# A mixture of 32 experts: the experts ordered on chip by their tokens, the 20 lightest four at a time in 32-slot column tiles

## The chip, the core and the metric

The kernel runs on one core of a Trainium2 chip. The core has a tensor engine (PE, with weight loads shown apart as PEld), a vector engine (DVE), a scalar engine (ACT), GpSimd (POOL), and SyncE (SP), which here issues the transfers; 16 DMA engines ("the rings") carry them. The metric is the device time of one execution in microseconds (us). A lower one is better.

## What the reference computes

Two transformer layers with attention mixers, feed-forward layers and norms over 256 tokens of 1024 features, in fp32, and at the end of the second layer a mixture of 32 experts (4 groups of 8). Each token takes the best group and in it the best two experts. All of the change lies in this mixture (shortened here):

```
pg_top, g_idx = lax.top_k(softmax(t @ w_rg + b_rg), 1)          # the group
le_sel = le[group g_idx of t @ w_re + b_re]
pe_top, e_idx = lax.top_k(softmax(le_sel), TOP_K)               # TOP_K = 2 of its 8 experts
pe_top = pe_top / jnp.sum(pe_top, axis=-1, keepdims=True)
flat_idx = g_idx * EXPERTS_PER_GROUP + e_idx
cw = jnp.sum(one_hot(flat_idx, 32) * (pg_top * pe_top)[..., None], axis=1)
for e in range(N_EXPERTS):
    he = jax.nn.silu(t @ w1e[e]) * (t @ w3e[e])                 # 1024 -> 256
    out = out + cw[:, e:e + 1] * (he @ w2e[e])                  # 256 -> 1024
```

So 512 pairs of token and expert are computed. The number of tokens of an expert follows from the inputs: with these, the heaviest have 34 and 33 tokens; of experts 6 to 31 the seventh heaviest has 21.

## The kernel before

The instructions are written in Python with a tile scheduler that orders each engine's instructions; pools of buffers with a tag ("ps", "we", ...) decide when a buffer can be reused. The mixture stage is `moe` with `moe_round`. It starts at about 1361 us of the span.

*Routing.* `moe` computes the router's choice on DVE, the number of tokens ahead of each token at its expert (a product with a triangle of ones into `pk`; its columns 64 to 95 are the tokens of each expert), the rank `rk` (token by expert: the slot of the token there, or a number far off) and the weights `cw`. If an expert has over 64 tokens, `n_more` further rounds follow; here there are none.

*Slots.* Each expert has CAP = 64 slots. `one_hot` makes for four experts the 0/1 matrix of tokens against 4 x 64 slots. `gather(qd)` multiplies the tokens (in a high and a low part, `hhi` and `hlo`) with it: `gT`, the tokens of four experts feature-major, in banks of the tag p0, read back by ACT and DVE.

*Passes.* There are N = 16 passes of two experts. `up(n)` multiplies the gathered tokens with w1 and w3: for each expert the 64 columns of `gT` are the stationary operand and go to 64 of PE's 128 columns, so that two experts stand beside one another and fill a bank (`ph`, tag p1) of 128 slots by 512. Behind it ACT and DVE form silu times the other half. `mid(n)` transposes the result and the slots' matrix; `down(n)` multiplies with w2, also two experts beside one another, into two banks; `scatter(n)` adds the slots' rows back to their tokens in four banks that stay for the whole stage. The order is written out by hand:

```
gather(0)
up(0)
for n in range(N):
    if n + 1 < N:
        up(n + 1)
    if n % 2 == 0 and n + 2 < N:
        gather(n // 2 + 1)
    mid(n)
    if n:
        scatter(n - 1)
    down(n)
```

*Weights.* An expert has 3 MB: two halves of w1|w3 together (`w13[e, 0]`, `w13[e, 1]`) and `w2e[e]`. Each MB is one transfer into a tile `we`, issued on SP. `expert_load(i)` gives the i-th MB in order of use, to a ring of 18 tiles from five pools; the first 18 are issued before the stage, the rest each when the tile's former contents (18 loads ago) have been used. All addresses are constants. The last two w2 come in four halves.

Of the kernel before, what the change touches and what calls it, by code (L numbers as in the profile page):

```python
# [33 lines left out]
KD = 8  # L34
# [5 lines left out]
CAP = 64  # L40
# [124 lines left out]
def interleave(gens, width, other=iter(()), every=1):  # L165
    """emit the steps of some units of work in turn, `width` units at a time, and every so often one of `other`"""
    gens, live, n = list(gens), [], 0
    while gens or live:
        while gens and len(live) < width:
            live.append(gens.pop(0))  # L170
        for g in list(live):
            if next(g, live) is live:
                live.remove(g)
            n += 1
            if n % every == 0:
                next(other, None)
    for _ in other:
        pass


class Net:
# [124 lines left out]
    def rope_steps(self, pool):  # L306
        """the rotary tables, as steps"""
# [41 lines left out]
    def split_w(self, src, n, cut=D, lo=None):  # L349
        """weights as hi and lo parts; returns col -> (hi, lo) accessor for column ranges within a half"""  # L350
# [31 lines left out]
    def split_a(self, src, pool=None, tag=None):  # L382
        """hi and lo parts of a [P, S] activation"""
# [37 lines left out]
    def prep(self, k, g):  # L421
        """operands of the next projection from the k-th chunk of x; the norm's factor comes later"""
# [20 lines left out]
    def bcast(self, cols, tag="p3"):  # L443
        """[P tokens, 2] factors -> [P, 2 * P tokens] on every partition (PSUM)"""
# [5 lines left out]
    def bcast_heads(self, out, cols):  # L450
        """[P tokens, (2, 2)] factors of two heads -> [(2 heads, 64), 2 * P tokens]"""
# [17 lines left out]
    def ffn(self, name, layer, post, side):  # L469
        """side(pool): steps of other work to lay between the chunks"""  # L470
# [56 lines left out]
    def feat(self, src, pairs, sink, count, tags=("p3",), lo=None):  # L527
        """feature-major projections, 128 columns at a time"""
# [10 lines left out]
    def gelu(self, out, h, k=1.0):  # L539
        """from x / 2: x * (1 + tanh(sqrt(2 / pi) * (x + 0.044715 * x**3))) / 2"""  # L540
# [29 lines left out]
    def rope_apply(self, raw, outs, key="h", swap=ROPE_SWAP):  # L570
        """outs: (tile slice, first partition, partitions)"""
# [52 lines left out]
    def out_proj(self, src, ys, post, order=tuple(range(KD))):  # L624
        """output projection: columns 0-511 accumulate as the chunks of ys come, in the given order"""
# [18 lines left out]
    def even_early(self):  # L644
        """what the even mixer needs that depends on weights and shapes only"""
# [212 lines left out]
    def odd_early(self):  # L858
        """the odd mixer's keys, with zeros for the other heads' features"""
# [127 lines left out]
    def ada_round(self, r, pool):  # L987
        """2048 of the modulation's columns, from c alone, as steps"""
# [27 lines left out]
    def prep_final1(self, k):  # L1016
        """sums of squares for the two norms that follow the last feed-forward of block 1"""
# [5 lines left out]
    def block2_early(self):  # L1023
        """operands of the third block that depend on weights alone, as steps"""
# [73 lines left out]
    def block2(self, post):  # L1098
        nc, A = self.nc, self.A
        rest = self.block2_in()  # L1100
        with self.tc.tile_pool(name="b2", bufs=1, reuse_waits="tile") as bp:
# [11 lines left out]
            def second(yl):  # L1113
                """the products with p_b, times their gates"""
# [155 lines left out]
    def lru_decay(self):  # L1270
        """4 * softplus(-lam) and its negative"""
# [61 lines left out]
    def rwkv_in(self, c, rkv, w2a, tw, half, hold):  # L1333
        """decays, keys and their products for two heads"""
# [92 lines left out]
    def pair_room(self, c, j):  # L1427
        """room for a unit in the weights' rings, which two units share"""
# [148 lines left out]
    def moe_pre(self):  # L1577
        """what the router needs besides x"""
# [11 lines left out]
        nc.sync.dma_start(self.lc, bass.AP(tensor=A["b_r"].tensor, offset=A["b_r"].offset, ap=[[0, P], [1, 36]]))  # L1590
        p = self.bank("p2")
# [4 lines left out]
    def post2(self, d, p, u):  # L1596
        """the mixers' part of x; router sums and token-major copies, without the norm's factor"""
# [21 lines left out]
    def keep_warm(self, n):  # L1619
        """products that nothing reads, so that the tensor engine's clock stays up while it waits"""  # L1620
# [4 lines left out]
    def moe(self, final):  # L1625
# [9 lines left out]
        with self.tc.tile_pool(name="moe", bufs=1, reuse_waits="tile") as mp:  # L1635
# [34 lines left out]
            def first_max(a, mx, shape):  # L1670
                """one-hot of the first of the largest entries"""
# [35 lines left out]
            self.rk = t(2, 32, keep=True)  # L1707
# [13 lines left out]
            self.tt(f2(self.rk), pk[:, 0:64], big, OP.add)  # L1721
# [23 lines left out]
            self.cw = t(2, 32, keep=True)  # L1745
# [7 lines left out]
            for i in range(3):  # L1753
                self.ts(th[:, i:i + 1], cm, CAP * (i + 1) + 0.5, op0=OP.is_gt)
# [5 lines left out]
            self.moe_round()  # L1760
            final()
            n_more = nc.values_load(nxi[0:1, 0:1], min_val=0, max_val=3)
            with self.tc.For_i(0, n_more, 1):
                rf = self.rk[:, :, :].rearrange("p j e -> p (j e)")
                self.ts(rf, rf, -float(CAP), op0=OP.add)
# [3 lines left out]

    def expert_open(self):  # L1770
        self.pre = self.es.enter_context(self.tc.tile_pool(name="pre", bufs=1, side="right", reuse_waits="tile"))
        self.rings, self.loads, self.ahead = [], 0, []
# [7 lines left out]
    def expert_ahead(self, n=99):  # L1780
        """start the loads of up to n more MB"""
        for _ in range(min(n, len(self.rings) - self.loads)):
            self.ahead.append(self.expert_load(self.loads))

    def expert_load(self, i):
        """the i-th MB of the experts' weights, in order of use: two experts' w1|w3 halves each time, and the w2 of the two before"""
        i %= 3 * NEXP
        if i < 4 or i >= 3 * NEXP - 2:
            n, i = (0, i) if i < 4 else (NEXP // 2 - 1, i - 3 * NEXP + 6)
        else:  # L1790
            n, i = (i - 4) // 6, (i - 4) % 6
            if i < 4:
                n += 1
# [325 lines left out]
```

## Time and profile before

| what | us |
|---|---|
| median of three timed runs | 1645.82 (1641.7 to 1648.69) |
| span of the profiled execution | 1641.5 |
| mixture stage, in the span | 1361 to 1641.5 |
| of it the 16 passes | 1376 to 1620 |

The profile is of one execution, and the page gives its span; its own device time lies around the span by some tenths of a us at most, as the fastest timed run of 1641.7 beside it shows. A row of the timeline has start, duration, engine, line of the kernel, operation, output and inputs by the program's names, and partitions x elements; "x16" are records that stand together, and in brackets is the idle time ahead and what ended it. fp32 products leave two records each. "SPq" is SP's queue of issues. The granted clock is a share of PE's full speed (2.4 GHz; 0.5 is 1.2).

### The profile page before, as it was taken

The page shows a single profiled execution, that of the slowest core. Times are in us where ns is not written, and L with a number is a line of the kernel's source. Part 1 is how long each engine was busy: PE and PEld are TensorE (multiplying, and loading weights), DVE is VectorE, ACT ScalarE, POOL GpSimd, SP SyncE. Part 2 cuts the span into 40 slices and gives each one's busy share as a digit, 9 for nine tenths or more (in the row PEclk, how much of TensorE's full clock was granted, in tenths as well). Part 3 has the DMA queues.
Part 4 walks back from the last instruction along what each step waited for, and adds up shares of the span by engine and source line. Part 5 has one row for each costly group of instructions (what it writes and reads, how often), then busy time and mean ns, then how long its engine had stood idle before and what let it go on. Part 6 is the DMA issues. An engine that isn't in the chain of part 4 may idle for free.

```text
span 1641.5 us, 29942 instructions
## 1 busy us (share of the span) xinstructions
PE 1580.0 (96%) x12048; PEld 1389.5 (85%) x12048; DVE 1069.2 (65%) x1964; ACT 709.7 (43%) x1263; POOL 321.0 (20%) x340
## 2 busy tenths in 40 slices
PE   8999998999999999999999999998999989999996
PEld 8999996789999999999879999997888886445443
DVE  6787776777876578757987777657875474323223
ACT  5544444545444444444554446544474332112112
POOL 4121222122221112112122221243231130000000
PEclk9999999999999999999999999999999999999998
DMA  8675554136765567555334775453431297999950
GB/s 300 246 276 197 202 195 156 52 129 212 276 217 174 187 234 275 207 172 185 116 107 163 271 269 180 142 203 105 156 116 53 81 377 291 405 422 420 387 205 28
DMA packets 61041, 344.33 MB, mean 210 GB/s; under 512 B 10976, under 2 KB 15200, under 8 KB 26848
## 3 DMA queue, kind: packets, MB, share of 16 engines
q1 hardware_dynamic: 58080, 340.65, 56.7%
q8 instruction: 96, 1.57, 0.4%
q0 software_dynamic: 640, 1.57, 0.4%
q10 hardware_dynamic: 2176, 0.13, 0.1%
q14 instruction: 49, 0.40, 0.1%
HBM read 339.05 MB, written 2.36 MB: 208 GB/s over the span
## 4 chain that ended last, share of the span: by engine, by line
PE 69%; issue 18%; DVE 8%; POOL 2%; ACT 2%; DMA 1%; SPq 0%; ACTq 0%; DVEq 0%; POOLq 0%
PE ps L232 68%; DVE l L238 2%; PE ps L235 1%; ACT h L257 1%; POOL rte L238 1%; DVE xl L247 0%; DVE t L238 0%; DVE xh L242 0%; POOL t L238 0%; DMA s<-in_ev_win 0%; DVE t L247 0%; POOL sq L238 0%; POOL kne L238 0%; DVE x L238 0%; DMA x<-in_xT 0%
## 5 line engine op out<-in xcount | busy, mean ns | idle before, releaser
L232 PE MATMUL ps<-xh,h 128*128 128x256 f32 x1992 | 568.3, 285 | 12.0 <-ACT h L257 5.9
L232 PE MATMUL ps<-xl,h 128*128 128x256 f32 x1992 | 567.2, 285 | 0.3
L232 PE MATMUL ps<-xh,l 128*128 128x256 f32 x1992 | 567.2, 285 | 0.2 <-DVE l L238 0.2
L257 ACT ACTIVATE h<-s 128x1024 fp32r<-128x1024 f32 (+4 forms) x419 | 401.4, 960 | 367.5 <-PE ps L232 289.1
L238 DVE TENSOR_TENSOR l<-s,h 128x1024 fp32r<-128x1024 f32 (+4 forms) x416 | 465.6, 1127 | 136.7 <-ACT h L257 135.2
L232 PEld LDWEIGHTS ps<-xh,h 128*128 128x128 f32 x1992 | 377.6, 190 | 17.0 <-ACT h L257 6.2
L232 PEld LDWEIGHTS ps<-xh,l 128*128 128x128 f32 x1992 | 378.6, 190 | 6.0 <-DVE l L238 1.9
L232 PEld LDWEIGHTS ps<-xl,h 128*128 128x128 f32 x1992 | 378.5, 190 | 1.7 <-DVE xl L247 1.1
L232 PE MATMUL ps<-ah,h 128*128 128x256 f32 x704 | 201.5, 286 | 0.0
L232 PE MATMUL ps<-ah,l 128*128 128x256 f32 x704 | 199.3, 283 | 0.1
L232 PE MATMUL ps<-al,h 128*128 128x256 f32 x704 | 199.1, 283 | 0.0
L238 POOL TENSOR_TENSOR t<-t,t 128x256 f32<-128x256 f32 x93 | 119.4, 1284 | 400.3 <-DVE t L238 340.8
L232 PEld LDWEIGHTS ps<-ah,l 128*128 128x128 f32 x704 | 134.9, 192 | 0.4 <-DVE l L238 0.3
L232 PEld LDWEIGHTS ps<-al,h 128*128 128x128 f32 x704 | 135.0, 192 | 0.0
L232 PEld LDWEIGHTS ps<-ah,h 128*128 128x128 f32 x704 | 134.9, 192 | 0.0
L232 PE MATMUL ps<-we,gT 128*64 128x512 f32 x512 | 122.9, 595 | 0.0
L238 DVE TENSOR_TENSOR t<-ps,rb 128x256 f32<-128x256 f32 x196 | 81.9, 420 | 33.2 <-PE ps L232 25.1
L232 PEld LDWEIGHTS ps<-we,gT 128*64 128x64 f32 x512 | 37.7, 137 | 71.3 <-issue 69.3
L257 ACT ACTIVATE ah<-t 128x256 fp32r<-128x256 f32 x88 | 36.7, 417 | 114.4 <-POOL t L238 114.4
L238 DVE TENSOR_TENSOR al<-t,ah 128x256 fp32r<-128x256 f32 x88 | 37.9, 431 | 61.8 <-ACT ah L257 61.8
L247 DVE SCALAR_TENSOR_TENSOR ada<-s,ca,ada 128x1024 f32<-128x1024 f32 x56 | 71.5, 1277 | 0.0
L238 POOL TENSOR_TENSOR sa<-sa,sq 128x256 f32<-128x256 f32 x34 | 41.8, 1230 | 149.9 <-ACT sq L257 149.4
(462 smaller groups left out, 2207.6 us busy)
## 6 DMA issues: line engine op xcount, KB each, us to landing
s<-in_ffn_gu SPq DMA_DIRECT2D x87, 1024.0 KB
we<-in_w SPq DMA_DIRECT2D x64, 1024.0 KB
s<-in_ffn_dn SPq DMA_DIRECT2D x64, 704.0 KB
we<-in_w2e SPq DMA_DIRECT2D x30, 1024.0 KB
s<-in_w_ada SPq DMA_DIRECT2D x24, 1024.0 KB
s<-in_w_in SPq DMA_DIRECT2D x18, 1024.0 KB
s<-in_w_ada_f SPq DMA_DIRECT2D x8, 1024.0 KB
s<-in_ev_win SPq DMA_DIRECT2D x7, 1024.0 KB
```

Source lines behind the costliest of these rows:

```text
L232: self.nc.tensor.matmul(out, lhsT, rhs, start=start, stop=stop, skip_group_check=True)
L235: self.nc.tensor.transpose(out, in_, ident)
L238: return (eng or self.nc.vector).tensor_tensor(out, a, b, op=op)
L247: self.nc.vector.scalar_tensor_tensor(out, a, s, b, op0=op0, op1=op1)
L257: self.nc.scalar.activation(out, a, f, **kw)
```

## The change

The 16 passes become 11: six of two experts with 64 slots for the positions 0 to 11, and five of four experts with 32 slots for 12 to 31. A position is not an expert's number any more: positions 0 to 5 are experts 0 to 5 (NFIX = 6), and behind them stand the others by their tokens, the heaviest first. `expert_order` computes this on DVE: a key of tokens x 32 less the number, for each expert how many keys are larger (its position), the one-hot `eq` of it, `ex` with the expert's number in it, and the permutation `perm`. `turn` then has two PE operations, which give each position's expert number (`idx`, copied as int32) and the transposed `rc` (ranks and weights); `place` multiplies with `perm`, for ranks and weights by position, `rcP`. From position 6 on, a weight load takes its address from a register: `value_load` reads `idx` into a register of SP (52 times, once for w13 and once for w2 of each position). A new `expert_list` gives the order of loads. `n_more` also counts if the seventh heaviest of experts 6 to 31 has over 32 tokens. Three small DVE operations in `moe_pre` prepare constants; docstrings are taken out. The sizes of the ring, the bytes and everything ahead of the stage stay. The core of the diff:

```diff
+NFIX, NWIDE = 6, 12
+PASSES = [(p, 2, 64) for p in range(0, NWIDE, 2)] + [(p, 4, 32) for p in range(NWIDE, NEXP, 4)]
...
-            self.rk = t(2, 32, keep=True)
+            self.rc = T("rc", (P, 4, 32))
+            self.rk, self.cw = self.rc[:, 0:2], self.rc[:, 2:4]
...
+            order = self.expert_order(T, pk[:, 64:96])
+            tn = t(3)
+            for i in range(3):
+                self.ts(tn[:, i:i + 1], self.top8[:, NWIDE - NFIX:NWIDE - NFIX + 1], 1024 * (i + 1) + 0.5, op0=OP.is_gt)
+            self.tt(th, th, tn, OP.max)
...
+    def expert_order(self, T, cnt):
...
+        self.stt(key, cnt, 32.0, iota, op0=OP.mult, op1=OP.subtract)
+        nc.vector.max(self.top8, key[:, NFIX:])
+        self.ts(key[:, 0:NFIX], iota[:, 0:NFIX], -1.0, 1.0e6, op0=OP.mult, op1=OP.add)
+        w = self.tmp("t2")
+        wq = w[:, 0:P].rearrange("p (q e) -> p q e", e=32)
+        self.tt(wq, idv, q4(key), OP.mult)
+        nc.vector.tensor_reduce(kp, w[:, 0:P], axis=AX.X, op=OP.add)
+        self.ts(gt, key, kp, op0=OP.is_gt)
+        nc.vector.tensor_reduce(pos, gt, axis=AX.X, op=OP.add)
+        self.ts(eq, iota, pos, op0=OP.is_equal)
+        self.ts(ex, eq, self.ei, op0=OP.mult)
+        perm = w[:, P:2 * P]
+        self.tt(perm.rearrange("p (q e) -> p q e", e=32), q4(eq), self.e4.unsqueeze(2).to_broadcast([P, 4, 32]), OP.mult)
+        def turn():
+            self.po = self.bank("p1")
+            self.mm(self.po[:, 0:32], self.ones[0:32, :], ex[0:32, :])
+            self.tr(self.po[:, P:2 * P], self.rc.rearrange("p a e -> p (a e)"), self.ident)
+            nc.vector.tensor_copy(self.idx, self.po[:, 0:32])
+            nc.vector.tensor_copy(rcT, self.po[:, P:2 * P])
+
+        def place():
+            self.mm(self.po[:, 2 * P:3 * P], rcT, perm)
+            nc.vector.tensor_copy(self.rcP.rearrange("p a e -> p (a e)"), self.po[:, 2 * P:3 * P])
...
+    def expert_list(self):
+
+        up = [[(0, p + i, h) for h in range(2) for i in range(n)] for p, n, _ in PASSES]
+        dn = [[(1, p + i, 0) for i in range(n)] for p, n, _ in PASSES]
+        return up[0] + up[1] + dn[0] + up[2] + dn[1] + dn[2] + up[3] + sum((u + d for u, d in zip(up[4:], dn[3:])), []) + dn[-1]
...
+        if p < NFIX:
+            src = self.A["w2e"][p] if kind else self.A["w13"][p, h]
+        else:
+            if (p, kind) not in self.where:
+                self.where[p, kind] = self.nc.sync.value_load(self.idx[0:1, p:p + 1], min_val=0, max_val=NEXP - 1)
+            e = bass.ds(self.where[p, kind], 1)
+            src = self.A["w2e"][e].squeeze(0) if kind else self.A["w13"][e, h].squeeze(0)
+        if kind and p >= PASSES[-1][0]:
+            self.late.append((t, src))
+            if len(self.late) == PASSES[-1][1]:
+                for c in range(2):
+                    for o, a in self.late:
+                        self.nc.sync.dma_start(o[:, c * D:(c + 1) * D], a[:, c * D:(c + 1) * D])
...
-            for k in range(KD):
-                for ee in range(2):
-                    c = (2 * (n % 2) + ee) * 64
-                    self.mm(ph[ee * 64:ee * 64 + 64, :], gT[k][:, c:c + 64],
-                            w[2 * ee + k // 4][:, (k % 4) * 512:(k % 4 + 1) * 512], k == 0, k == KD - 1)
+            for h in range(2):
+                w = self.expert_get(*[(0, p + i, h) for i in range(m)])
+                for k in range(4):
+                    for i in range(m):
+                        c = n % 2 * P + i * cap
+                        self.mm(ph[i * cap:(i + 1) * cap, :], gT[4 * h + k][:, c:c + cap], w[i][:, k * 512:(k + 1) * 512], h == 0 and k == 0, h == 1 and k == 3)
...
-                    for ee in range(2):
-                        self.mm(py[ee * 64:ee * 64 + 64, :], heT[:, f * P + ee * 64:f * P + ee * 64 + 64],
-                                w[ee][:, nn * D + f * 512:nn * D + (f + 1) * 512], f == 0, f == 1)
+                    for i in range(m):
+                        self.mm(py[i * cap:(i + 1) * cap, :], heT[:, f * P + i * cap:f * P + (i + 1) * cap],
+                                w[i][:, nn * D + f * 512:nn * D + (f + 1) * 512], f == 0, f == 1)
...
-        N = NEXP // 2
+        N = len(PASSES)
         gather(0)
+        turn()
         up(0)
+        place()
```

The order of instructions on PE at the start of the stage, before: gather(0)'s products (stationary `oh`) with the first products of up(0) (stationary `gT`, moving `we`) between them.

```order
L232 MATMUL ps_16976<-oh_3166_16910,hlo_16902 128x256
L232 MATMUL ps_16998<-we_16260,gT_16946 64x512
L232 MATMUL ps_16998<-we_15207,gT_16947 64x512
L232 MATMUL ps_16998<-we_16260,gT_16947 64x512
L232 MATMUL ps_16998<-we_15207,gT_16948 64x512
L232 MATMUL ps_16987<-oh_3165_16909,hhi_16899 128x256
L232 MATMUL ps_16987<-oh_3165_16909,hlo_16901 128x256
```

The same place of the change: the end of gather(0), the two operations of `turn` (`moe_ex`, `moe_rc`), and then up(0) from its first product.

```order
L233 MATMUL ps_17011<-oh_3167_16916,hlo_16908 128x256
L233 LDWEIGHTS ones
L233 MATMUL ps_17022<-moe_ex,ones 128x32
L236 MATMUL ps_17022<-con,moe_rc 128x128
L233 MATMUL ps_17027<-we_15207,gT_16970 64x512
L233 MATMUL ps_17027<-we_15209,gT_16970 64x512
L233 MATMUL ps_17027<-we_15207,gT_16971 64x512
```

All of gather(0) now stands ahead of up(0), with the products of `turn` between the two.

A down on PE before, in the middle of the stage: two banks (17519 and 17526) one after the other, two experts (`we`) in turn.

```order
L232 MATMUL ps_17519<-we_17515,t_3293_17493 64x512
L232 MATMUL ps_17519<-we_17517,t_3293_17493 64x512
L232 MATMUL ps_17519<-we_17515,t_3293_17493 64x512
L232 MATMUL ps_17519<-we_17517,t_3293_17493 64x512
L232 MATMUL ps_17526<-we_17515,t_3293_17493 64x512
```

A down of a narrow pass of the change: two banks (18030, 18041) and four experts (`we_17986`, `_17997`, `_18008`, `_18019`).

```order
L233 MATMUL ps_18030<-we_17986,t_3353_17964 32x512
L233 MATMUL ps_18041<-we_17986,t_3353_17964 32x512
L233 MATMUL ps_18030<-we_17997,t_3353_17964 32x512
L233 MATMUL ps_18041<-we_17997,t_3353_17964 32x512
L233 MATMUL ps_18030<-we_18008,t_3353_17964 32x512
L233 MATMUL ps_18041<-we_18008,t_3353_17964 32x512
L233 MATMUL ps_18030<-we_18019,t_3353_17964 32x512
L233 MATMUL ps_18030<-we_17986,t_3353_17964 32x512
L233 MATMUL ps_18030<-we_17997,t_3353_17964 32x512
```

The two banks alternate for the first three experts, so that neighbouring products there have the same expert and the same columns of PE.

SP's order in the change, where the loads by register begin (`ISA` are register operations); before, this is a row of DMA issues with nothing between.

```order
L1864 DMA we_16812<-in_w2e 128x2048
L1854 TENSOR_LOAD moe_idx
L1854 ISA x2
L1864 ISA
L1864 DMA we_17223<-in_w 128x2048
L1854 TENSOR_LOAD moe_idx
L1854 ISA x2
L1864 ISA
L1864 DMA we_17234<-in_w 128x2048
```

Ahead of each load of a new expert stand a TENSOR_LOAD and three register operations on SP.

## Rows read from the trace of the kernel before

**Rows 1.** The page: span, and busy time of each engine (share of the span, instructions).

```profile
span 1641.5 us, 29942 instructions
PE 1580.0 (96%) x12048; PEld 1389.5 (85%) x12048; DVE 1069.2 (65%) x1964; ACT 709.7 (43%) x1263; POOL 321.0 (20%) x340
```

**Rows 2.** Windows: length, PE, PEld, DVE, ACT, POOL busy, clock, DMA share, GB/s.

```profile
1370.00:1380.00 10.00, 10.00 (x55) 5.07 (x55) 5.31 (x29) 4.66 (x8) 0.00 (x0) 1.00 0.19 64
...
1405.00:1435.00 30.00, 30.00 (x169) 15.35 (x169) 9.25 (x22) 5.44 (x11) 0.00 (x0) 1.00 1.01 423
1435.00:1465.00 30.00, 30.00 (x170) 15.33 (x170) 9.25 (x22) 5.42 (x11) 0.00 (x0) 1.00 1.01 421
...
1376.00:1622.00 246.00, 243.55 (x1301) 119.77 (x1299) 71.24 (x168) 43.99 (x81) 0.23 (x1) 1.00 0.82 333
...
1582.00:1584.00 2.00, 1.92 (x10) 0.91 (x12) 0.84 (x3) 0.00 (x0) 0.00 (x0) 1.00 0.21 86
```

**Rows 3.** Timeline of PE and its weight loads, 1450 to 1475 us (start, duration).

```profile
1454.38 3.65 PE L232 MATMUL ps<-we,t 128*64 128x512 f32 x16
...
1454.86 0.14 PEld L232 LDWEIGHTS ps<-we,t 128*64 128x64 f32 x2 [0.29 <-issue]
...
1457.86 7.04 PE L232 MATMUL ps<-we,gT 128*64 128x512 f32 x32
...
1465.56 0.28 PE L232 MATMUL ps<-t,yh 128*128 128x256 f32 x1
1465.68 0.28 PE L232 MATMUL ps<-t,yl 128*128 128x256 f32 x1
```

**Rows 4.** Timeline of SP: issues of weight loads in the mixture stage.

```profile
1377.45 3.79 SPq L1805 DMA_DIRECT2D we<-in_w  x2
...
1428.06 0.80 SPq L1805 DMA_DIRECT2D we<-in_w2e  x2
...
1458.06 1.58 SPq L1805 DMA_DIRECT2D we<-in_w2e  x2
...
1574.15 2.92 SPq L1803 DMA_DIRECT2D we<-in_w2e  x4
```

**Rows 5.** Waits of SP, 1325 to 1641 us: total, times, longest.

```profile
SPq L1805 <- PE ps L232: 168.8, 44, 14.6
```

**Rows 6.** Timeline of DVE around the first gather.

```profile
1370.95 0.48 DVE L242 TENSOR_SCALAR gT<-ps,mod 128x256 f32<-128x256 f32 x1
...
1371.60 0.41 DVE L238 TENSOR_TENSOR oh<-con,moe_r 128x256 fp32r<-128x256 f32 x1
...
1372.52 0.15 DVE L1757 CAST moe_nxi<-t 128x1 int32<-128x1 f32 x1
...
1372.92 0.47 DVE L242 TENSOR_SCALAR gT<-ps,mod 128x256 f32<-128x256 f32 x1
```

**Rows 7.** Timeline of PE around the first gather.

```profile
1375.17 0.39 PE L232 MATMUL ps<-oh,hhi 128*128 128x256 f32 x1
...
1376.33 12.23 PE L232 MATMUL ps<-we,gT 128*64 128x512 f32 x54
```

**Rows 8.** Timeline of all engines at the end.

```profile
1616.34 3.65 PE L232 MATMUL ps<-we,t 128*64 128x512 f32 x16
...
1629.84 3.12 SPq L1938 DMA_DIRECT2D out<-o  x5
```

**Rows 9.** Instructions of line 1762, and of tile we: ns min/median/max, first and last start.

```profile
L1762 SPq TENSOR_LOAD <-moe_nxi x1: 468/468/468, 1577.1 to 1577.1; - x1
L1762 SPq FUSED_REGOPS  x1: 186/186/186, 1577.7 to 1577.7; - x1
...
L1805 SPq DMA_DIRECT2D we<-in_w x64: 327/328/1755, 1197.8 to 1563.2; - x64
```

**Rows 10.** A window of an earlier stage, and PE's timeline in it.

```profile
1200.00:1210.00 10.00, 7.75 (x29) 4.55 (x28) 9.06 (x22) 9.44 (x18) 2.62 (x4) 0.83 0.51 205
...
1206.27 1.96 PE L232 MATMUL ps<-t,rgw 128*128 128x256 f32 x4 [1.00 <-DVE t L247]
```

More of the change, by code (lines that the diff above doesn't have):

```diff
@@ L1744, in moe @@
             self.tt(w2, w1, e2, OP.mult)
-            self.cw = t(2, 32, keep=True)
             for j in range(2):
@@ L1758, in moe @@
             es.close()
-            self.moe_round()
+            self.moe_round(*order)
             final()
@@ L1763, in moe @@
             with self.tc.For_i(0, n_more, 1):
-                rf = self.rk[:, :, :].rearrange("p j e -> p (j e)")
-                self.ts(rf, rf, -float(CAP), op0=OP.add)
+                self.ts(self.rk, self.rk, -64.0, op0=OP.add)
+                for c, cap in ((slice(0, NWIDE), 64.0), (slice(NWIDE, NEXP), 32.0)):
+                    a = self.rcP[:, 0:2, c]
+                    self.ts(a, a, -cap, op0=OP.add)
                 self.one_hot(0)
@@ L1768, in moe @@
                 final()
+    def expert_order(self, T, cnt):
+        nc = self.nc
+        iota = self.C("iota")[:, 0:32]
+        idv = self.ident.rearrange("p (q e) -> p q e", e=32)
+        q4 = lambda a: a.unsqueeze(1).to_broadcast([P, 4, 32])
+        rcT = self.tmp("t3")
+        key, gt, eq, self.top8, kp, pos = (rcT[:, a:a + n] for a, n in ((128, 32), (160, 32), (192, 32), (224, 8), (232, 1), (233, 1)))
+        rcT = rcT[:, 0:P]
+        ex = T("ex", (P, 32), BF)
+        self.idx = T("idx", (P, 32), I32)
+        self.rcP = T("rcP", (P, 4, 32))
+        self.stt(key, cnt, 32.0, iota, op0=OP.mult, op1=OP.subtract)
[20 more added lines that the diff above has]
+            nc.vector.tensor_copy(self.rcP.rearrange("p a e -> p (a e)"), self.po[:, 2 * P:3 * P])
+        return turn, place
     def expert_open(self):
         self.pre = self.es.enter_context(self.tc.tile_pool(name="pre", bufs=1, side="right", reuse_waits="tile"))
-        self.rings, self.loads, self.ahead = [], 0, []
+        self.rings, self.loads, self.ahead, self.where, self.late = [], 0, {}, {}, []
         self.expert_ring(NEARLY, "wa")
@@ L1804, in expert_load @@
+        if kind and p >= PASSES[-1][0]:
[4 more added lines that the diff above has]
+                        self.nc.sync.dma_start(o[:, c * D:(c + 1) * D], a[:, c * D:(c + 1) * D])
         else:
             self.nc.sync.dma_start(t, src)
-        return t
-    def expert_next(self, n):
-        return [self.ahead.pop(0) if self.ahead else self.expert_load(self.loads) for _ in range(n)]
@@ L1811, in one_hot, with expert_get @@
-    def one_hot(self, qd):
-        es = slice(4 * qd, 4 * qd + 4)
-        self.oh[qd] = [self.ptmp(f"oh{j}", (P, 4, CAP), F32R, bufs=2) for j in range(2)]
+        return (kind, p, h), t
+    def expert_get(self, *keys):
+        for k in keys:
+            while k not in self.ahead:
+                k2, t = self.expert_load(self.loads)
+                self.ahead[k2] = t
+        return [self.ahead.pop(k) for k in keys]
+    def one_hot(self, b):
+        of = PASSES[2 * b:2 * b + 2]
+        p0, n, cap = of[0][0], sum(q[1] for q in of), of[0][2]
+        rk = self.rcP[:, 0:2] if b else self.rk
+        self.oh[b] = [self.ptmp(f"oh{j}", (P, S), F32R, bufs=2) for j in range(2)]
@@ L1821, in moe_round, with gather @@
         nc, A = self.nc, self.A
+        self.where, self.late = {}, []
         acc = [self.bank(t) for t in ("p2", "p2", "p3", "p3")]
         ohs, gTs, hes, mids = self.oh, {}, {}, {}
-        def gather(qd):
-            if qd:
-                self.one_hot(qd)
-            oh = ohs[qd]
-            gT = gTs[qd] = [self.xp.tile([P, S], F32, tag=f"xh{k}", name=self.name("gT")) for k in range(KD)]
+        def gather(b):
+            if b:
+                self.one_hot(b)
+            w = P * len(PASSES[2 * b:2 * b + 2])
+            gT = gTs[b] = [self.xp.tile([P, S], F32, tag=f"xh{k}", name=self.name("gT")) for k in range(KD)]
@@ L1874, in down @@
         def down(n):
-            heT, _, cs = mids[n]
-            w = self.expert_next(2)
+            (heT, _, cs), (p, m, cap) = mids[n], PASSES[n]
+            w = self.expert_get(*[(1, p + i, 0) for i in range(m)])
             for nn in range(2):
```

52 lines of the change are left out of this document (23 added, 29 removed).

## The prediction

> **What bounds the kernel now.** The page's totals come first [rows 1]: TensorE (PE) is busy for 1580.0 of 1641.5 us, so the reader should look for what else is full at the same time. The change touches only the mixture stage, which runs from about 1361 us to the end; so the next view is the table by windows [rows 2]. Between 1376 and 1622 PE is busy for 243.55 of 246 us at a granted clock of 1.00, so it is the bound there. But the same rows have a second full resource: in 1405 to 1465 the DMA share is 1.01 at 421 to 423 GB/s. In 1582 to 1584 it is 0.21, 0.42 us of work, so the last byte of weights is there at 1582.4. Both are explained by SyncE's (SP's) timeline [rows 4]: two passes are 12 loads of 1 MB, and their w2 loads go out at 1428.06 and 1458.06, every 30.0 us. That is 12.58 MB in 30.0 us, or 419 GB/s: PE's pace and the DMA rings' own pace are equal to a per cent. SP waits for PE to give a slot back, 168.8 us in 44 waits [rows 5], yet the rings always hold work that is already issued. What PE has ahead of the rings' end is therefore only the 18 MB of the ring: the last four half loads go out from 1574.15 for 2.92 us [rows 4], and PE works on what lies in the ring until the last down ends, 1616.34 + 3.65 = 1619.99 [rows 8]. **So that end stands 37.6 us behind the last byte, and this is all that a faster PE can win while the bytes stay.** Behind the down come 21.5 us of scatter, norm and output, whose last stores go out from 1629.84 [rows 8], to 1641.5.
>
> **The change, term by term.** Bytes: 96 MB before and after, 18 issued ahead and 78 from the ring (333 GB/s x 246 us = 81.9 MB = 78 x 1.0486 [rows 2]). At 421 GB/s a load takes 2.49 us and 78 take 194 us.
>
> *PE's work.* A pair of 64-column tiles starts every 0.42 us (0.14 of weight load and 0.28 idle [rows 3]) and PE's records show an up of 7.04 us and a down of 3.65 for two experts; scatter and gather products follow one another at 0.12 us [rows 3], so 16 of a scatter cost 1.9 and a pass's half of 32 gather products 1.9; four transposes and the changes of form add 0.5. Sum: 15.0 us, half of the 30.0 above. Six such passes stay (90 us). Ten others become five with four 32-column tiles. No row shows four at once. Lower bound: all four in the time of two, 7.04 for up. Upper bound: two at a time, 14.1. I take the lower for up, since the nearest row, the pair, shows full overlap. For down the order on PE counts: the products of the two output banks alternate, so that neighbours want the same columns (the excerpt of a narrow down); I count seven groups of 0.86 us for what could be four, 6.0 in place of 3.65. A narrow pass is then 7.0 + 6.0 + 1.9 + 1.9 + 0.5 and some changes of form, 18 us. Five are 90, against 150 for what they replace: 60 us less work on PE, more than the 37.6 us there are to win.
>
> *The start.* Ahead of the second gT write DVE gets about fifteen small operations of expert_order, in the place where rows show 0.15 to 0.48 each [rows 6], 3 to 4 us; the bank that gather(0) needs back is freed by those gT writes. The two products of turn() stand behind all of gather(0) and ahead of up(0) in PE's order (the excerpts of the start), so the 10 records of up(0) that now run between gather's products no longer do, and the products wait for the last of expert_order. Today gather resumes at 1375.17 and ups run from 1376.33 [rows 7]; I put up(0) at 1378. The first slots come free after half of it, 1381.5, against 1377.45 today [rows 4]: 4 us. Until then the rings have little to do, as today (0.19 in 1370 to 1380 [rows 2]). Bounds: 1 us (if the scheduler's order hides it) to 8 (if all of it comes one after another). place() needs one product and one copy behind up(0), both beside up(1): nothing; without that cover 0.8 us, by a product at 0.39 [rows 7] and a DVE write at 0.41 [rows 6].
>
> *The rings after that.* Loads 19 to 34 are released as today plus 4 us and take 16 x 2.49 = 40 us. The new list puts the w2 of three passes ahead of up(3)'s weights, so loads 35 and 36 reuse the slots of down(2), which are given back at 1428.06 + 4 = 1432 [rows 4]. The rings are idle for about 10 us in all until then. From 1432 on 62 loads wait for no PE work that is late, 62 x 2.49 = 154.4, with the flight of the last 1588. Bounds: 1581 (no idle time) to 1594 (idle twice). PE meanwhile ends its wide passes at 1378 + 90 = 1468 and would need until 1558 for the narrow ones; it is 30 us early and will wait for weights: DMA becomes the bound.
>
> *SP.* Fifty-two value loads: one costs 468 ns of TENSOR_LOAD and some 0.2 of register work behind it, as the one at the end does [rows 9]; 84 issues stay at 0.33. That is 36 + 28 = 64 us, with the extra instruction ahead of each perhaps 75, of 200 us: hidden beside the transfers. Lower bound nothing, upper the third rival.
>
> *The end.* The last four w2 come as eight halves, so behind the last byte half a down is left, 8 records, 1.7 us, and then the 21.5 us: 1588 + 1.7 + 21.5 = 1611. PE comes out of waits there. After gaps of about 1 us the rows show a stretch at 0.83 mean clock, in which four products of 0.28 take 1.96 us [rows 10]. I add 4.5 us for a last pass that lags at the low level (the work behind the last bytes doubles and the last up's tail is behind too): 1616. Bounds: 0 and 10.
>
> **Sum.** 1616 against 1641.5, -25.5 us. The three timed runs before are 1641.7 to 1648.69; on their median of 1645.82 it is **1620 us**.
>
> **Rivals.**
> *Two tiles at a time.* The four 32-column tiles run as two pairs. Up 14.1, down 7.3, the rest 6.3: 27.7 a pass, 1468 + 138.5 = 1606.5, with waits 1610, and no byte is late any more; 1610 + 21.5 + 2 = 1633.5, on the median 1638. For it: nothing in the trace runs more than two. Against it: the overlap of the pair is complete. Chance 0.13, half of it beyond 0.5%. Strictly one at a time (1790) would deny even the pairs.
>
> *The clock, on the other side.* In the narrow stage PE waits for a load every 2.5 us, and the rows of the earlier stage show the low level after gaps of 1 us [rows 10]. At the low level a narrow pass takes 36 us, more than the 30 that its bytes take: 1468 + 180 + 4 + 21.7 = 1674, on the median **1678, slower**. It decides by the mean clock of the stage: at 0.75 PE just keeps up (1468 + 90/0.75 = 1588); at 0.58 nothing of the gain is left. Against it: a PE that is late doesn't wait, and in all of today's stage without waits the clock is 1.00. Chance 0.16: 0.05 faster, 0.03 same, 0.08 slower.
>
> *SP's register loads.* If a value load costs much more while loads are queued (a flush, a wait for the copy to moe_idx), SP issues too late. It has to pay 154 us for 62 loads; over 2.5 us a load it is the bound, and at 3.1 the gain is gone (62 x 0.6 = 37). For it: some issues take up to 1755 ns today [rows 9]; against it their median of 328. Chance 0.05, mostly slower.
>
> *The rings don't hold 421.* A slower transfer of all 78 loads moves the last byte by itself. The gain is gone where that byte is there at 1641.5 - 23.2 = 1618.3; less 1381.5 and 11 us of idle time and flight this leaves 225.8 us, 2.89 a load or 362 GB/s. The lowest figure of the rows is the stage's mean of 333, which holds the idle ends; against it stand 421 and 423 in whole windows of 30 us [rows 2], with loads of the same shape. The time would be 1641.5, on the median 1646. Chance 0.03, same. The Trainium skill gives some 358 GB/s as the limit of HBM for one core (DMA: Bandwidth & Descriptors, Specifications); by it the last byte would be there at about 1621, an estimate, and the change would be worth nothing. The trace disagrees by 18%.
>
> Beside these, 0.05 that it goes better than 1606 (no idle of the rings, no lag). A further round of the experts happens only if the order leaves one with over 32 tokens behind position 12 or any has over 64; by the counts that the inputs give (the seventh heaviest behind the six fixed has 21, the heaviest 34) none does.
>
> For the four tiles at once the Trainium skill has a measured speedup of 2.38 for three column tiles of 32 (TensorE: Matmul & The Clock Gate, Measured speedup vs the span model); by that an up would take about 8.8 us in place of 7.0, an estimate, and a narrow pass 21: still under the 30 us of its bytes. No run here shows it yet.
>
> **How the numbers follow.** Forecast 0.58; two tiles 0.13; clock 0.16; SP 0.05; rate 0.03; better 0.05. Timed runs here spread by 0.2% to either side, so 0.5% (under 1637.6, over 1654) is about what can be told from no change. Faster: 0.58 + 0.06 + 0.05 + 0.01 + 0.05 = 0.75. Same: 0.07 + 0.03 + 0.03 = 0.13. Slower: 0.08 + 0.04 = 0.12. The forecast's own range is 1610 to 1632, from the bounds of start (-3 to +4), rings (-7 to +6) and end (-4.5 to +5.5). For 8 in 10 I take 1606 to 1642: it takes in two tiles at a time and part of the low clock, and leaves out most of the slower cases.
>
> **What would show it.** Right: the DMA share near 1.0 from about 1432 to 1588 with a gap ahead of it; PE's idle time in front of 32-column products ended by weights; four products of 32 columns to 0.86 us in ups and fewer in downs; the first load by register at about 1381; TENSOR_LOADs of about 0.5 us; the last down 2 to 7 us behind the last byte. Wrong: PE busy through the narrow stage (tiles in pairs, or a clock at 0.5), rings idle while SP works or waits on a register, or an end that stays more than 10 us behind the last byte.

## The result, and the profile after

| | before | after |
|---|---|---|
| median, us | 1646.2 (4 runs, 1641.7 to 1648.69) | 1624.66 (4 runs; 1623.47 of the three that the ratio uses) |
| ratio to before | | 0.9868, 95% interval [0.9837, 0.9898] |
| span of the profiled execution, us | 1641.5 | 1621.6 |
| first product of gather(0) | 1368.5 | 1369.9 |
| last packet of weights | 1583.2 | 1592.5 |
| end of the last down | 1620.0 | 1600.7 |
| stage, gather(0) to the end | 273.0 | 251.7 |

The change is worth some 22 us, 1.3% (21.7 us by the ratio); 1620 was predicted. Three of the four runs lie between 1620.24 and 1625.85 us; one ran at a lower clock throughout and took 2026.08, and the ratio leaves it out. The time at which gather(0) begins moves by several us from one profile to the next (1363.4 to 1373.9 over all runs below) although hardly anything ahead of it is changed, so the stages are compared from there on.

First the page of the changed kernel, its span and busy times.

```profile
span 1621.6 us, 29873 instructions
PE 1540.0 (95%) x11888; PEld 1360.5 (84%) x11888; DVE 1049.3 (65%) x1932; ACT 697.2 (43%) x1240; POOL 321.3 (20%) x340
```

Then its windows, with the columns of [rows 2].

```profile
1376.00:1380.00 4.00, 1.97 (x8) 0.69 (x10) 2.41 (x12) 1.74 (x2) 0.00 (x0) 0.83 0.00 0
1380.00:1400.00 20.00, 19.62 (x98) 8.71 (x94) 2.86 (x8) 2.19 (x5) 0.00 (x0) 0.95 0.74 284
...
1428.00:1432.00 4.00, 4.00 (x31) 3.17 (x31) 3.04 (x9) 0.81 (x2) 0.00 (x0) 1.00 0.02 6
1432.00:1436.00 4.00, 4.00 (x21) 1.29 (x18) 1.32 (x2) 1.37 (x2) 0.00 (x0) 1.00 0.21 33
...
1470.00:1500.00 30.00, 28.91 (x201) 13.87 (x203) 6.77 (x18) 4.04 (x8) 0.00 (x0) 1.00 1.01 420
1500.00:1530.00 30.00, 23.93 (x139) 8.40 (x132) 4.82 (x10) 3.09 (x5) 0.00 (x0) 1.00 1.01 421
1530.00:1560.00 30.00, 26.49 (x155) 11.83 (x154) 6.03 (x17) 3.23 (x7) 0.00 (x0) 1.00 1.01 419
1560.00:1580.00 20.00, 15.02 (x71) 3.56 (x70) 0.42 (x1) 0.38 (x1) 0.00 (x0) 0.83 1.01 423
...
1590.00:1592.00 2.00, 1.98 (x15) 0.39 (x7) 0.06 (x1) 0.69 (x1) 0.00 (x0) 1.00 0.69 279
1592.00:1594.00 2.00, 1.60 (x8) 1.06 (x9) 1.18 (x2) 0.07 (x1) 0.00 (x0) 1.00 0.06 25
...
1590.00:1600.00 10.00, 8.71 (x51) 4.08 (x44) 1.72 (x3) 2.97 (x7) 1.46 (x2) 1.00 0.15 61
```

From 1440 to 1580 the rings are full (a share of 1.01, 419 to 423 GB/s), and from 1470 on PE has gaps beside that: the bound has moved from PE to the bytes. Ahead of it lies a hole at 1428 to 1436, in which the rings are nearly idle (0.02 and 0.21). SP's timeline shows what ends it.

```profile
1383.78 12.23 SPq L1864 DMA_DIRECT2D we<-in_w  x8
...
1417.55 1.58 SPq L1864 DMA_DIRECT2D we<-in_w2e  x2
1434.60 5.97 SPq L1864 DMA_DIRECT2D we<-in_w  x8
```

SP has nothing to issue from 1419 to 1434.60, when down(2) has given its slots back. What its register loads cost stands with their line, as in [rows 9].

```profile
L1854 SPq TENSOR_LOAD <-moe_idx x52: 262/269/464, 1378.7 to 1565.2; - x52
L1854 SPq FUSED_REGOPS  x52: 147/152/177, 1379.2 to 1565.5; - x52
```

Last PE's own timeline: the start, a narrow pass, waits for weights, and the end.

```profile
1369.94 0.28 PE L233 MATMUL ps<-oh,hhi 128*128 128x256 f32 x1
...
1378.03 0.18 PE L233 MATMUL ps<-moe_ex,ones 32*128 32x32 bf16 x1 [2.08 <-DVE moe_ex L243]
...
1378.40 8.78 PE L233 MATMUL ps<-we,gT 128*64 128x512 f32 x32
...
1484.48 3.64 PE L233 MATMUL ps<-we,gT 128*32 128x512 f32 x32
...
1496.34 3.95 PE L233 MATMUL ps<-we,t 128*32 128x512 f32 x29 [0.81 <-issue]
...
1500.09 0.64 PE L233 MATMUL ps<-we,t 128*32 128x512 f32 x3
...
1510.61 1.05 PE L233 MATMUL ps<-we,gT 128*32 128x512 f32 x2 [1.43 <-DMA we<-in_w]
1513.10 3.19 PE L233 MATMUL ps<-we,gT 128*32 128x512 f32 x25 [1.44 <-DMA we<-in_w]
...
1595.89 0.61 PE L233 MATMUL ps<-mean,sq 128*128 128x1 f32 x4 [0.87 <-ACT sq L258]
1596.42 1.05 PE L233 MATMUL ps<-we,t 128*32 128x512 f32 x2
1597.40 1.50 PE L233 MATMUL ps<-mean,sq 128*128 128x1 f32 x12
1598.83 1.90 PE L233 MATMUL ps<-we,t 128*32 128x512 f32 x10
```

32 records of 32 columns take 3.64 us where 32 of 64 columns took 7.04 [rows 3]: four tiles do run at once. The waits for weights are there: 14 of them from 1470 to 1593, 13.1 us in all, none over 1.44. And at the end PE does the last down in pieces, with sums of squares (`mean,sq`) between, 4 to 8 us behind the last byte.

### The profile page after: what moved, and what is told of

Read it like the earlier page. It is cut to its first block, busy times and chain, and to the rows that moved or that the text cites. A ratio compares the mean times of both kernels' runs of the same rounds, so it can differ in the third digit from the quotient of the medians.

```text
span 1621.6 us, 29873 instructions
## 1 busy us (share of the span) xinstructions
PE 1540.0 (95%) x11888; PEld 1360.5 (84%) x11888; DVE 1049.3 (65%) x1932; ACT 697.2 (43%) x1240; POOL 321.3 (20%) x340
## 4 chain that ended last, share of the span: by engine, by line
PE 76%; DVE 8%; DMA 8%; issue 3%; POOL 2%; ACT 2%; SPq 0%; ACTq 0%; DVEq 0%; POOLq 0%
PE ps L233 75%; DMA we<-in_w 5%; DMA we<-in_w2e 2%; DVE l L239 2%; PE ps L236 1%; ACT h L258 1%; DVE t L239 1%; POOL rte L239 1%; DVE xl L248 1%; DVE xh L243 0%; POOL t L239 0%; DMA s<-in_ev_win 0%; DVE t L248 0%; POOL sq L239 0%; POOL kne L239 0%
## 5 line engine op out<-in xcount | busy, mean ns | idle before, releaser
L233 PE MATMUL ps<-we,gT 128*32 128x512 f32 (+1 forms) x512 | 100.6, 620 | 10.1 <-DMA we<-in_w 9.7
L233 PEld LDWEIGHTS ps<-we,gT 128*32 128x32 f32 (+1 forms) x512 | 26.7, 124 | 66.1 <-issue 46.0
```

Source lines behind the costliest of these rows:

```text
L233: self.nc.tensor.matmul(out, lhsT, rhs, start=start, stop=stop, skip_group_check=True)
```

## The experiments

Each ratio is to the kernel before. Two runs that lie close together are compared by the stage in the profile of one execution each; where their intervals overlap, the difference rests on these two profiles.

**Constant addresses.** What do SP's register loads cost?

```diff
-            if (p, kind) not in self.where:
-                self.where[p, kind] = self.nc.sync.value_load(self.idx[0:1, p:p + 1], min_val=0, max_val=NEXP - 1)
-            e = bass.ds(self.where[p, kind], 1)
-            src = self.A["w2e"][e].squeeze(0) if kind else self.A["w13"][e, h].squeeze(0)
+            src = self.A["w2e"][p] if kind else self.A["w13"][p, h]
```

> The changed kernel with constant addresses for all weight loads: position p reads expert p, so the 26 positions behind the fixed ones are given weights of other experts than their tokens belong to; the work, the bytes and the order of everything else stay. Theory (SP's register loads are hidden beside the transfers): the same time as the change, 1620 to 1626 us, within 2 us; the rings' idle time around 1430 and the last byte stay where they are. Rival (52 register loads, 0.27 + 0.15 us each and a register move ahead of each issue, hold the rings up): 5 us or more faster, and a DMA share that has no dips behind 1440 that the change has.

1623.98 us, ratio 0.9866 [0.985, 0.9883]; stage 251.5 us. They cost nothing: 52 value loads of 0.27 + 0.15 us and 82 issues lie beside the transfers. The rival falls.

**Half of the bytes in the narrow stage.**

```diff
-            self.nc.sync.dma_start(t, src)
+            c = D if p >= NWIDE else 2 * D
+            self.nc.sync.dma_start(t[:, :c], src[:, :c])
```

The last pass's halves are cut to quarters in the same way, and the narrow products read `k % 2` for `k`.

> The changed kernel with half of the bytes for the 20 narrow experts: each weight load there brings only the first half of its columns, and the products use that half twice, so that the result is not that of the reference; the number of loads, products and everything else stay. Theory (in the narrow stage the rings' bytes are the bound and four tiles run at once): the last byte is there at about 1515, PE becomes the bound again with 16 to 18 us a narrow pass, the end comes 40 to 50 us earlier than in the change, a time of 1572 to 1585 us. Rival 1 (tiles run two at a time, 27.7 us a pass, or the clock is low when PE is loaded): the time falls by under 10 us. Rival 2 (issue of the loads on SP or their number is the bound): the time falls by under 10 us too, but with PE waiting.

1578.18 us, 0.9582 [0.9565, 0.9599]. Its windows:

```profile
1470.00:1500.00 30.00, 30.00 (x237) 15.37 (x234) 10.47 (x27) 5.42 (x10) 0.00 (x0) 1.00 0.94 344
1500.00:1530.00 30.00, 29.20 (x211) 13.46 (x213) 5.06 (x13) 3.62 (x8) 0.00 (x0) 1.00 0.90 339
```

PE is busy nearly throughout again at a clock of 1.00 and waits for no load. The last packet of weights comes at 1538 and not at 1515, as the expectation had it. On its timeline an up of four experts, in one piece, is 64 records:

```profile
1476.07 7.07 PE L233 MATMUL ps<-we,gT 128*32 128x512 f32 x64
```

The downs of four narrow passes begin at 1489.68, 1503.79, 1527.12 and 1542.28, so three passes take 52.6 us, 17.5 each. They are not alike: a gather stands only in every second pass, and the two without one take 14.1 and 15.2 us, the one with it 23.3, with its up in pieces. Some 46 us lie between the change and this run, time that the change spends behind bytes, and both rivals of this run fall.

**The hole at 1430.** Eight fixed positions, and the plain order of loads:

```diff
-NFIX, NWIDE = 6, 12
+NFIX, NWIDE = 8, 12
...
-        return up[0] + up[1] + dn[0] + up[2] + dn[1] + dn[2] + up[3] + sum((u + d for u, d in zip(up[4:], dn[3:])), []) + dn[-1]
+        return up[0] + sum((u + d for u, d in zip(up[1:], dn)), []) + dn[-1]
```

> The changed kernel with eight fixed positions in place of six and the loads in plain order of use (the weights of up(3) ahead of the w2 of pass 2), so that the 18 loads ahead of the stage end with half of up(3) and the 35th load reuses a slot of up(3), not of down(2). Theory (the rings stand idle for about 8 us, 1427 to 1435, for the slots of down(2), and this moves the last byte): the idle time there is under 2 us, the last byte 6 to 8 us earlier, the time 6 to 8 us below that of the change, 1616 to 1619 us. Rival (what is lost there is caught up later, or another slot is late in its place): within 2 us of the change.

1616.71 us, 0.9822 [0.9806, 0.9839]; the stage is 244.8 us, 6.9 shorter. Its window over the hole:

```profile
1424.00:1436.00 12.00, 12.00 (x71) 6.33 (x71) 4.76 (x12) 2.32 (x4) 0.00 (x0) 1.00 1.01 421
```

The rings are full there, and the last packet comes 214.3 us behind gather(0), where the change has 222.6. By the windows the rings' idle time behind the first load is 2.9 us, where the change has 9.8, so here 6.9 us less of idle time make the stage 6.9 us shorter: about one for one. Which of the two edits does it was not tried apart.

**The order at the end.** PE's sums of squares behind the last down, ACT's squares behind the last yh:

```diff
+        with self.tc.issue_after(self.last.ins):
             self.sums_tok([q for k, q in enumerate(sq) if k - 1 not in X_ADD], p)
...
+            with self.tc.issue_after(self.out_yh.ins):
                 self.act(sq[-1], self.x[k], AF.Square)
```

(`self.last` is the last product of a down, `self.out_yh` its last read-out; the two copies ahead of the squares are kept back too.)

> The changed kernel with the norm's products and squares at the end kept behind the last down and its read-out: the sums of squares behind the last down's last product in PE's order, and the squares and copies behind the last yh in ACT's. Theory (at the end PE stands in its own order behind sums that wait for ACT's squares, while the last weights have been there since 1591.4): the last down ends 2 to 3 us behind the last byte and no longer 9, the time is 4 to 7 us below that of the change, 1617 to 1621 us. Rival (the end is long because PE's clock is low there, or because the squares have to be made anyway): within 2 us of the change, with the down earlier and the sums as late as before.

1621.75 us, 0.9849 [0.9833, 0.9866]. The last down ends 4.3 us behind the last packet, not 8.2, but from that packet to the end it is 26.7 us for 29.1: only 2.4 won, and the intervals of this run and of the change overlap. The sums are later now and run at the low clock (0.50 from 1603.2 to 1607.6):

```profile
1603.21 4.43 PE L233 MATMUL ps<-mean,sq 128*128 128x1 f32 x20 [0.52 <-ACT sq L258]
```

The theory holds in its place and not in its size; the rival's part of it (the sums have to be made anyway) is real.

**Both, with the last pass written out.** As in the two runs before, and for the last pass half a down, its scatter, the other half, its scatter:

```diff
+            down(n, (0, 1) if n < N - 1 else (0,))
+        scatter(N - 1, range(4))
+        with self.tc.issue_after(self.sc.ins):
+            down(N - 1, (1,))
+            scatter(N - 1, range(4, 8))
```

> Eight fixed positions with loads in order of use, and at the end the last pass written out: first half of the down, its scatter, second half of the down, its scatter, then the sums of squares, with ACT's squares behind the last yh. Theory (8 us of idle rings and some 5 us of PE's order at the end are two separate losses, and both lie on the path): 1610 to 1614 us, the last down's end 3 to 4 us behind the last byte. Rival (the order at the end gains nothing because the sums then run at the low clock): 1615 to 1618 us, as with eight fixed positions alone.

1610.97 us (6 runs), 0.9799 [0.9785, 0.9812]. The last half in one piece:

```profile
1578.83 1.92 PE L233 MATMUL ps<-we,t 128*32 128x512 f32 x16
...
1584.31 2.39 PE L233 MATMUL ps<-mean,sq 128*128 128x1 f32 x20 [0.52 <-ACT sq L258]
```

It ends 3.0 us behind the last packet (1577.7), and the sums are done at full clock, 2.39 us for 4.43. Why the clock holds here is open: in the 8 us ahead of the sums PE is idle for 2.85 us, more than the 2.07 of the run before, and in the next run, which has the same end, the clock falls while the sums run, and they take 3.26. From packet to end it is 23.7 us, 30.6 with eight fixed positions alone; the stage is 6.8 us shorter than there, the median 5.7.

**The start.** On top of that, the order of the experts is worked out behind gather(0), `turn` comes behind up(0) and `place` behind up(1):

```diff
         gather(0)
-        turn()
         up(0)
+        turn()
+        up(1)
         place()
         for n in range(N):
-            if n + 1 < N:
+            if 0 < n < N - 1:
                 up(n + 1)
```

(All of `expert_order` behind the key moves into `turn`; its bank is one of p0.)

> The kernel of the run before this one in which the order of the experts is worked out behind gather(0) and up(0), turn between up(0) and up(1) and place behind up(1); with eight fixed positions no load needs it before the 23rd. Theory (DVE's added operations and turn hold up(0) back by 3 to 4 us and the low clock behind it costs 1, and since the rings are the bound from there on, that moves the last byte): first load from the ring at 1377 to 1379 us, the time 3 to 4 us below that run, 1606 to 1611 us. Rival (the wait at the start is caught up while the rings still work through the first loads): within 1.5 us of that run.

1609.12 us (5 runs), 0.9776 [0.9762, 0.979]. The first load from the ring is issued 9.7 us behind gather(0), nearly as before the change (8.9), in place of 13.8. But the last packet is only 2.0 us earlier against gather(0), since the rings then stand still a little longer for down(0)'s slots:

```profile
1400.00:1420.00 20.00, 20.00 (x100) 8.04 (x100) 6.58 (x16) 3.13 (x5) 0.00 (x0) 1.00 0.81 326
```

The gain of 1.9 us on the median (1.1 in the stage) lies between theory and rival, and the intervals of the two runs just overlap: the first load is 4 us earlier, and half of that is lost again in the next 40. This is the fastest version here that loads all the bytes, 2.2% below the kernel before.

**The order and the registers alone, with all passes wide.**

```diff
-PASSES = [(p, 2, 64) for p in range(0, NWIDE, 2)] + [(p, 4, 32) for p in range(NWIDE, NEXP, 4)]
+PASSES = [(p, 2, 64) for p in range(0, NEXP, 2)]
```

> The changed kernel with all 16 passes of two experts and 64 slots, so the order by tokens, turn, place, the register loads and the new list of loads without the narrow tiles. Theory (only the narrow tiles win; PE is the bound again and the start is 2 to 4 us later): 1645 to 1651 us, no gain on the kernel before and up to 0.3% slower, the last byte of weights 35 us ahead of the last down as before. Rival (the order or the list of loads has a part in the gain): under 1640 us.

1661.03 us, 1.0092 [1.0076, 1.0107]: slower by 15 us, and neither side had that. PE waits for no weights in it. Two passes take 30.0 us at first, as in the kernel before, and 36.0 from 1525 on (downs at 1525.37, 1561.41, 1597.46). SP's timeline shows it too:

```profile
1529.01 1.50 SPq L1864 DMA_DIRECT2D we<-in_w2e  x2
...
1565.06 1.50 SPq L1864 DMA_DIRECT2D we<-in_w2e  x2
```

The next runs show where that comes from.

**The kernel before with half of the bytes.** (The same cut for experts 12 to 31.)

> The kernel before with half of the bytes for the experts 12 to 31: each load brings the first half of its columns and the products use it twice, so the result is not that of the reference; loads and products keep their number. Theory (before, PE alone is the bound and the rings' bytes are free): 1643 to 1649 us, no change, with the DMA share of the later windows near 0.5. Rival (the rings at 1.01 are a bound of the kernel before too): 10 us or more faster.

1636.19 us, 0.9942 [0.9924, 0.996]: 9.5 us faster, which the theory denied; and the rival's reason doesn't hold either, for in the kernel before PE waits for no load. With this one in hand the kernel before reads differently. SP's timeline shows two passes in 33.3 us from 1519 on, which [rows 4] had at 30.0:

```profile
1519.08 0.80 SPq L1805 DMA_DIRECT2D we<-in_w2e  x2
...
1552.40 0.80 SPq L1805 DMA_DIRECT2D we<-in_w2e  x2
```

PE's timeline of the kernel before in that stretch has an up in pieces, 2 records and 30, with gather and scatter between:

```profile
1533.92 1.07 PE L232 MATMUL ps<-we,gT 128*64 128x512 f32 x2
1537.96 7.08 PE L232 MATMUL ps<-we,gT 128*64 128x512 f32 x30
```

With half of the bytes the scheduler that writes the order put each up in one piece, and two passes took 30.0 to the end.

**PE in the written order**, with the bytes as they are. Each part of the loop is kept behind the last product of the part ahead:

```diff
+        def then(f, k):
+            with self.tc.issue_after(self.last.ins):
+                f(k)
+
         for n in range(N):
             if n + 1 < N:
-                up(n + 1)
+                then(up, n + 1)
...
-            down(n)
+            then(down, n)
```

On the kernel before:

> The kernel before with PE kept in the written order within the loop: each up, gather, mid, scatter and down only behind the last product of the one ahead of it. Theory (from about 1500 us the kernel before loses 3.3 us in every two passes because PE's order breaks ups into pieces between gather and scatter products, and each change of form costs; no bytes are late): 30.0 us for two passes to the end, 1634 to 1639 us. Rival (the passes of 33.3 us are weights that come late): PE waits for loads in the same places, 1643 us or more.

1638.63 us (9 runs), 0.9963 [0.9951, 0.9974]. The same place as above:

```profile
1530.69 3.70 PE L232 MATMUL ps<-we,t 128*64 128x512 f32 x16
1534.17 7.09 PE L232 MATMUL ps<-we,gT 128*64 128x512 f32 x32
```

Two passes take 30.2 us to the end and no load is waited for. So some 6 us of the kernel before are pieces in PE's order and not bytes: 5.7 on the median, and the stage goes from 273.0 to 266.2. With half of the bytes it was 264.3, and most of what is left between the two is that a pair of passes took 30.0 there.

On the all-wide version:

> The change with 16 passes of two experts (so without narrow tiles) and PE kept in the written order within the loop. Theory (the 15 us that the all-wide version lost against the kernel before are 6 us of a later start and 9 us and more of a more broken order of PE): 30.0 us for two passes to the end, 5 to 7 us more than the kernel before in the written order, 1639 to 1645 us. Rival (the order by tokens, the register loads or the list of loads cost something in every pass): over 1650 us.

1642.81 us (10 runs), 0.9989 [0.9976, 1.0002]: 18 us below the all-wide version, and in the stage 5.0 above the kernel before in the written order (271.2 against 266.2). Two passes take 30.2 or 30.3 us:

```profile
1529.80 1.50 SPq L1864 DMA_DIRECT2D we<-in_w2e  x2
...
1560.11 1.51 SPq L1864 DMA_DIRECT2D we<-in_w2e  x2
```

So the 5.0 us are the start (first load 13.8 us behind gather(0), not 8.9), and the order by tokens and the register loads cost nothing in every pass.

On the change itself:

> The changed kernel with PE kept in the written order within the loop. Theory (from 1440 us on the rings are the bound, so PE's order is hidden there, and in the wide passes ahead of that it is hardly broken): within 3 us of the change, 1622 to 1627 us. Rival (PE's broken order sets the end here as well): 5 us or more faster.

1621.08 us, 0.9856 [0.9835, 0.9877], 1 us under the range expected; the intervals of this run and of the change overlap, and in its profile the stage is 253.9 us for 251.7. Here, where the rings are the bound, PE's order makes no difference that can be told.

## Why the prediction was right, point by point

**The bound moves to the bytes** (37.6 us are all there is to win): right. By the last packet, at 1583.2 and not at the 1582.4 that was read from a mean share, it is 36.8, and the best version here takes 36.1 us off the stage (236.9 for 273.0). The DMA share is 1.01 or 1.02 from 1440 to 1590; halving the bytes brings some 46 us more, and the constant addresses nothing.

**PE's work.** A narrow pass was put at 18 us; it takes 17.5 in the mean where no bytes are late. That the two agree is luck: the down was put too long, so that a pass without a gather takes 14.1 or 15.2 us where the terms give 16.1, and the pieces in PE's order were left out, so that one with a gather takes 23.3 where they give 19.9. Four tiles at once was right: an up takes 7.07. The Trainium skill's 2.38 for three column tiles (TensorE: Matmul & The Clock Gate, Measured speedup vs the span model) would have made 8.8 us of an up, an estimate; the trace has 7.07 and decides. For down the count of seven groups of 0.86 was wrong: the down at 1496.34 stands in the order that I counted as 6.0, and from its first record to the end of its last three at 1500.73 it takes 4.4 us, 29 of the 32 records in 3.95. Two halves with the columns in turn take 1.92 each. So in that order the products of one column tile hardly hold up the other tiles: it costs half a us, not two. A second slip was in what is replaced: ten wide passes cost 150 us only at 15.0; from 1515 on they cost 16.6 in the kernel before, for the pieces in PE's order. None of this moved the forecast, for PE was not the bound.

**The start**: up(0) at 1378, measured 1378.40; first load at 1381.5, measured 1383.78. Behind the 2.08 us in front of `turn`'s product the clock fell (0.83 in 1376 to 1380, 0.95 in 1380 to 1400), so up(0) took 8.8 us where 7.0 were counted, and the first load goes out 5.4 us behind its start, not 3.5. In the run with the other start, which has no such wait, it was 1.00 from 1370 to 1390. Of the 4 us put down here, 2 reach the last packet, by that run.

**The rings**: 10 us of idle time, measured 9.8 behind the first load (1.4, 0.8, 2.1 and 5.5 in the windows of 1383.78 to 1400, 1400 to 1410, 1420 to 1430 and 1430 to 1440), 7.6 of them around the hole that eight fixed positions close. 62 loads of 2.49 us from 1432 on made 1588; the 35th load went out at 1434.60, 2.6 us later, and the last packet landed at 1592.5, 4.5 later; the other 1.9 were not traced. The Trainium skill's limit of some 358 GB/s for one core (DMA: Bandwidth & Descriptors, Specifications) is not what bounds these loads: the trace has 419 to 423 from 1440 to 1580.

**The end** was the term that was mis-sized: 1.7 + 4.5 us from the last byte to the last down; 8.2 were measured. The step put it down to the low clock. The clock was 1.00 in 1590 to 1600. The runs showed another cause: sums of squares in PE's order ahead of the last down, behind which it waits for ACT. With the sums kept behind the down it is 4.3, with the last pass written out 3.0.

**The clock, the rival on the other side**: it had to bring the mean of the narrow stage under 0.75. It was 1.00 in 1470 to 1560 and 0.83 for the next 20 us, so the rival did not come. **SP's loads** cost 0.27 + 0.15 us, not 0.47 + 0.19. **Two tiles at a time** and **a lower rate** are excluded by the rows above.

**Slips that changed nothing**: half a down is 16 records of 1.92 us in all, not 8 and 1.7; there are 82 issues, not 84; the rest of a narrow pass is 5.0 us in its own sum and 6.3 in that of two tiles at a time; and the bounds of start, rings and end add up to 1605.5 to 1635.5, not to 1610 to 1632.

The sum made the end 1588 + 1.7 + 21.5 + 4.5 = 1615.7 on the span; it was 1621.6. The 5.9 us are 4.5 at the last packet (1.4 of them there when gather(0) begins) and 2.0 from it to the last down, less 0.6 in the rest (20.9 for 21.5).

## What to carry to other kernels

Where two resources are both full, the gain from freeing one is the lead that it has on the other at the end, not the work saved: here some 37 us of about 60, less what the change itself costs. Once transfers were the bound here, 7 us in which the queue was empty counted in full: look at the order of loads against the order in which slots come back, and at what stands behind the last byte in the engines' own orders. Halve the bytes to see the other bound, but look at whether the order of instructions changed with them.

## What the runs showed that was not expected

- Products that share 32 columns and stand next to one another hardly hold up the other columns: such a down took 4.4 us, 29 of its 32 records in 3.95; half a down with the columns in turn took 1.92 for 16.
- Pieces in PE's order are dear: in the all-wide version two passes took 36.0 us in the scheduler's order and 30.2 in the written one, with the same products, and PE is shown busy nearly throughout in both. Counted by the starts of PE's records, the form (64 columns or 128) changes 3 times in two passes of 30.0 or 30.2 us, 7 or 8 times in those of 33.3 in the kernel before, and 13 or 14 times in those of 36.0: 0.55 to 0.8 us for each further change, by these rows.
- Eight waits for weights of 0.5 to 1.44 us left the granted clock at 1.00 from 1500 to 1560; waits of 1.44, 1.34 and 1.44 (at 1563.00, 1567.97 and 1570.45) stand in the 20 us at 0.83, and one of 2.08 ahead of up(0) stands in the 4 us at 0.83 (1376 to 1380).
